# MLP second product as seven block products of Strassen's kind in three of four pairs of groups

## The chip, the cores and the metric

The kernel runs on one core of a Trainium2 chip. The metric is device microseconds (us) of one execution, lower is better. Three runs of the kernel before took 1183.5, 1185.58 and 1185.76 us, so its median is 1185.58 us. The profile is of one further execution.

## The reference, cut to what matters

A decoder trunk of two layers on 512 tokens of width 1024, all in fp32. Layer 0 mixes with gated linear attention, layer 1 with stick-breaking attention; behind each mixer and behind each MLP stands a LayerNorm on `ALPHA * h + mix`. The change touches the MLP alone, which is the same in both layers:

```python
D_MODEL = 1024
SEQ = 512
D_FF = 4 * D_MODEL
...
def sq_relu_mlp(x, w_up, w_down):
    h = jax.nn.relu(x @ w_up)
    return (h * h) @ w_down
...
        h = layer_norm(DEEPNORM_ALPHA * h + sq_relu_mlp(h, mlp_w_up[layer], mlp_w_down[layer]),
                       ln_g[layer, 1], ln_b[layer, 1])
```

The second product is (512 tokens x 4096 features) by (4096 features x 1024 columns).

## The kernel before, in words

**Three matmuls for one product.** Operands are kept as two fp32r parts: `hi` is the value rounded by ScalarE (ACT), `lo` is the rest, subtracted by VectorE (DVE). `mm3` (L85 to L89) sums hi x hi, hi x lo and lo x hi in one PSUM bank. A weight piece is 512 KB: `split_piece` (L62) loads it with SyncE's queue (SP) into one of 3 `raw` buffers, ACT writes `hi` (L67), DVE writes `lo` (L69), 128 x 1024 elements each, into 6 buffers of either kind. `put` (L91) does the same for a computed tile.

**The MLP.** `mlp` (L513) cuts the 4096 features into 8 groups of 512. `up(g)` (L522) makes a group: 96 matmuls of 128 x 512 (four weight pieces, four banks), relu on ACT (L540), the square on DVE (L541) and the split by `put` into 128 x 512 pieces. `down(g)` (L545) takes two groups, a pair: for each half of the 1024 columns it loads four pieces, and sums over both groups in four banks, one per 128 tokens, 12 matmuls per group and bank. So a pair's `down` has 192 matmuls and eight pieces. When a bank is done, DVE adds it to the rows `h` of the residual stream (L161; L159 for the first pair, which scales by ALPHA too), eight adds a pair. The order is up 0, 1, 2, down of pair 0, up 3, up 4, down of pair 2, and so on (L586 to L594): one `up` always lies between a group's matmuls and the `down` that reads it. The last pair is different, since the LayerNorm follows each 128 tokens there.

**What sets the order.** The code is recorded by a framework with a scheduler; each engine then runs its list strictly in order, and tile pools make an instruction wait for the last user of a buffer. PSUM has 8 banks, all from one pool (L53). `unit` (L58) gives 8 buffers of four 128 x 512 tiles, tag `T`; four of them hold the MLP's input. 

Of the kernel before, what the change touches and what calls it, by code (L numbers as in the profile page):

```python
# [34 lines left out]
def yoco_kernel(ctx: ExitStack, tc: tile.TileContext, x, gla_w_in, gla_w_a2, gla_b_a, gla_norm_g,  # L35
                gla_w_o, kv_w, sb_w_q, sb_w_o, mlp_w_up, mlp_w_down, ln_g, ln_b, out):
    nc = tc.nc
# [10 lines left out]
    def nm(s):  # L48
        uid[0] += 1
        return f"{s}{uid[0]}"  # L50

    def bank():
        return psp.tile([P, 512], F32, tag="b", name=nm("ps"))  # L53

    def row_tile():
        return big.tile([P, D], F32, tag="h", bufs=4, name=nm("h"))

    def unit(dtype):  # L58
        return big.tile([P, 4, 512], dtype, tag="T", bufs=8, name=nm("T"))


    def split_piece(src, a):  # L62
        raw = wts.tile([P, 1024], F32, tag="raw", bufs=3, name=nm("raw"))
        v = lambda w: w.rearrange("p (a b) -> p a b", a=a)
        nc.sync.dma_start(out=v(raw), in_=src)
        hi = wts.tile([P, 1024], F32R, tag="hi", bufs=6, name=nm("hi"))
        nc.scalar.activation(hi, raw, AF.Copy)  # L67
        lo = wts.tile([P, 1024], F32R, tag="lo", bufs=6, name=nm("lo"))
        nc.vector.tensor_tensor(lo, raw, hi.bitcast(F32), op=ALU.subtract)  # L69
        return v(hi), v(lo)  # L70

    def pieces_512(w, r0, nkt, c0):

        got = []
        for kp in range(nkt // 2):
            hi, lo = split_piece(
                w[r0 + 256 * kp:r0 + 256 * kp + 256, c0:c0 + 512].rearrange("(a p) c -> p a c", p=P), 2)
            got += [(hi[:, 0, :], lo[:, 0, :]), (hi[:, 1, :], lo[:, 1, :])]
        return got

    def piece_128(w, c0):
        hi, lo = split_piece(w[:, c0:c0 + 128].rearrange("(a p) c -> p a c", p=P), 8)
        return [(hi[:, k, :], lo[:, k, :]) for k in range(8)]

    def mm3(ps, a, b, first, last):  # L85

        nc.tensor.matmul(ps, lhsT=a[0], rhs=b[0], start=first, stop=False)  # L87
        nc.tensor.matmul(ps, lhsT=a[0], rhs=b[1], start=False, stop=False)  # L88
        nc.tensor.matmul(ps, lhsT=a[1], rhs=b[0], start=False, stop=last)  # L89

    def put(hi, lo, ps, keep=lambda ins: ins):  # L91
        keep(nc.scalar.activation(hi, ps, AF.Copy))
        keep(nc.vector.tensor_tensor(lo, ps, hi.bitcast(F32), op=ALU.subtract))  # L93
# [191 lines left out]
    xs, pss = [row_tile() for _ in range(NT)], [bank() for _ in range(NT)]  # L285
    pcs = []
# [7 lines left out]
    for u in range(2):  # L294
        for t in range(NT):
            nc.sync.dma_start(out=xs[t][:, 512 * u:512 * u + 512],
                              in_=x2[128 * t:128 * t + 128, 512 * u:512 * u + 512])
# [3 lines left out]
            raw, hi, lo = (w[:, 512 * (t % 2):512 * (t % 2) + 512] for w in trio)  # L301
            k = 4 * u + t
# [19 lines left out]
    for k in range(8):  # L322
# [3 lines left out]
    a1 = gtp.tile([P, S], F32R, name="a1")  # L326
    nc.scalar.activation(a1[:CH, :], ps[:CH, :], AF.Identity, bias=onerow)
    nc.vector.scalar_tensor_tensor(a1[CH:, :], ps[:CH, :], onerow, a1[:CH, :].bitcast(F32), op0=ALU.add,
                                   op1=ALU.subtract)
    pcs = pieces_512(w_in, 0, 8, 2 * QK + 512)  # L330
    for h in range(GH):
        ps = rows(xT, h, pcs, K8)
        put(vT[1][0][:, h, :], vT[1][1][:, h, :], ps)
        ps = bank()
        c = slice(128 * h, 128 * h + 128)
# [151 lines left out]
    onT.grow()  # L487
    gate(0, 1, pcs)
# [6 lines left out]
    hs = [Rows() for _ in range(NT)]  # L495
# [3 lines left out]
    pcs = pieces_512(gla_w_o[0], 0, 8, 0)  # L499
# [5 lines left out]
    pcs = pieces_512(gla_w_o[0], 0, 8, 512)  # L505
# [5 lines left out]
    NG = DFF // 512  # L511

    def mlp(l, hT, late, vec, done):  # L513


        ml = tc.tile_pool(name=nm("mlp"), bufs=1, reuse_waits="tile")
        mlp_ = ml.__enter__()

        def work():
            return mlp_.tile([P, 512], F32, tag="w2", bufs=6, name=nm("w"))  # L520

        def up(g):  # L522
            pcs = pieces_512(mlp_w_up[l], 0, 8, 512 * g)
            pss = [bank() for _ in range(4)]
            for c0, cn in ((0, 256), (256, 256)) if g == 0 else ((0, 512),):
                for k in range(8):
                    if g == 0 and c0 == 0 and k == 4:
                        late(work)
                    for f in range(4):
                        mm3(pss[f][:, c0:c0 + cn], tuple(w[:, 128 * f:128 * f + 128] for w in pcs[k]),  # L530
                            hT.k(k, c0, cn), k == 0, k == 7)
            if g % 3 == 2:
                sq = Split(0)
                for parts in (sq.hi, sq.lo):
                    parts.append(mlp_.tile([P, 4, 512], F32R, tag="U", bufs=2, name=nm("U")))
            else:
                sq = Split(1)
            for f in range(4):
                r, s2 = work(), work()
                nc.scalar.activation(r, pss[f], AF.Relu)  # L540
                nc.vector.tensor_tensor(s2, pss[f], r, op=ALU.mult)  # L541
                put(sq.hi[0][:, f, :], sq.lo[0][:, f, :], s2)
            return sq

        def down(g, sqs):  # L545

            first, last = g == 0, g == NG - 2

            def into(ps, t, i, pcs, c=slice(0, 512)):
                for k in range(4):  # L550
                    mm3(ps, sqs[i].k(k, 128 * t, 128), tuple(w[:, c] for w in pcs[4 * i + k]),
                        (i, k) == (0, 0), (i, k) == (1, 3))

            for n in range(1 if last else 2):
                pcs = pieces_512(mlp_w_down[l], 512 * g, 8, 512 * n)
                pss = [bank() for _ in range(NT)]
                for i in range(2):
                    for t in range(NT):
                        into(pss[t], t, i, pcs)
                        if i == 1:  # L560
                            hs[t].add(n, pss[t], first, last and not (l == 1 and t == NT - 1))
                            if last and l == 1 and t == NT - 1:
                                for q in range(2):
                                    hs[t].stat(0, q, hs[t].h[:, 256 * q:256 * q + 256], 2)
            if not last:
                return None
            pcs = pieces_512(mlp_w_down[l], 512 * g, 8, 512)

            def mm(t):
                if l == 0 or t < NT - 1:  # L570
                    ps = bank()
                    for i in range(2):
                        into(ps, t, i, pcs)
                    hs[t].add(1, ps, False, True)
                    return

                for q in range(2):
                    ps = bank()[:, 0:256]
                    for i in range(2):
                        into(ps, t, i, pcs, slice(256 * q, 256 * q + 256))  # L580
                    h = hs[t].h[:, 512 + 256 * q:768 + 256 * q]
                    nc.vector.tensor_tensor(h, ps, h, op=ALU.add)
                    hs[t].stat(1, q, h, 2)
            return done(mm, work)

        sqs = [up(0), up(1)]  # L586
        for h in hs:
            h.affine(vec)
        for g in range(0, NG, 2):
            if g + 2 < NG:  # L590
                sqs.append(up(g + 2))
            got = down(g, sqs[g:g + 2])
            if g + 3 < NG:
                sqs.append(up(g + 3))  # L594
        ml.__exit__(None, None, None)
        return got

# [2 lines left out]
    def done0(mm, work):  # L600
        h2T.grow()
        h2T.grow()
        return finish(mm, lncols(0, 1), hs, h2T, work)

    late = mlp(0, hT, late, vec, done0)


# [22 lines left out]
    for n in range(2):  # L630
        pcs = pieces_512(kv_w, 0, 8, D + 512 * n)
# [88 lines left out]
    parts = [(oA.hi[0][:, i, :], oA.lo[0][:, i, :]) for i in range(4)]  # L720
# [6 lines left out]
    for p in range(NP):  # L727
# [4 lines left out]
        else:  # L732
            n = p - (NP - 2)
            pcs = pieces_512(sb_w_o[0], 0, 4, 512 * n)
# [29 lines left out]
    def done1(mm, work):  # L764
# [40 lines left out]
```

## Time and profile before

| what | value |
|---|---|
| profiled execution, device time | 1185.81 us |
| its span, first to last instruction | 1183.9 us |
| granted TensorE clock, mean | 0.999 |
| TensorE (PE) busy | 1167.5 us, 99% of the span, 5629 instructions |
| VectorE (DVE) busy | 635.1 us, 54%, 846 instructions |
| ScalarE (ACT) busy | 458.7 us, 39%, 754 instructions |
| GpSimd (POOL) busy | 96.5 us, 8%, 159 instructions |
| memory traffic | 112.41 MB in DMA packets, mean 95 GB/s |
| DVE's share in the middle of layer 0's MLP (296 to 340 us) | 18.19 of 44.00 us |

How to read it: the profile gives for each engine its busy time, and for each group of instructions the source line, the mean duration and what ended the idle time ahead of them. Matmuls are pipelined, so one lasts longer than the distance to the next; what counts is the distance from start to start. In rows of the profile, `out<-in` names tiles without their numbers, `128*128 128x512` is the weight tile and then the output's partitions and elements.

### The profile page before, as it was taken

Reading aid. Unit: us, or ns where it says so; the run is one execution under the profiler, and the core shown is the slowest. Engines: PE = TensorE matmul, PEld = TensorE weight load, DVE = VectorE, ACT = ScalarE, POOL = GpSimd, SP = SyncE. Lnnn points to the kernel's source line nnn. Section 1 sums busy time; section 2 is a strip of 40 time slices with the busy share of each in tenths; the row PEclk is TensorE's granted clock in tenths of the full one; section 3 lists DMA queues with packets and bytes.
Section 4 is the critical chain, followed back from the end, with each engine's and each line's share of the span. In section 5 each row is a group of like instructions: output and inputs, shape, how many; then the busy total and the mean of one; then the engine's idle time right before and its main releaser. Section 6 shows DMA issues by size and latency. Waiting matters only on the chain.

```text
span 1183.9 us, 14158 instructions
## 1 busy us (share of the span) xinstructions
PE 1167.5 (99%) x5629; PEld 967.8 (82%) x5629; DVE 635.1 (54%) x846; ACT 458.7 (39%) x754; POOL 96.5 (8%) x159
## 2 busy tenths in 40 slices
PE   8999999999999999999999999999999999999997
PEld 7788888898888888888888877778988888888886
DVE  4577545753434434335735878778734344244346
ACT  4455333543323224223635666755433133233220
POOL 1011100100000000000101444330000000000001
PEclk9999999999999999999999999999999999999999
DMA  7441124342333232232244121211532322323212
GB/s 228 122 125 54 36 90 149 99 143 92 102 93 107 89 105 91 89 107 86 75 125 125 54 71 38 71 36 38 177 107 73 119 94 89 108 90 99 96 36 71
DMA packets 82949, 112.41 MB, mean 95 GB/s; under 512 B 11010, under 2 KB 36738, under 8 KB 82884
## 3 DMA queue, kind: packets, MB, share of 16 engines
q1 hardware_dynamic: 82884, 111.52, 30.7%
q8 instruction: 44, 0.72, 0.3%
q14 instruction: 21, 0.17, 0.0%
HBM read 109.41 MB, written 2.10 MB: 94 GB/s over the span
## 4 chain that ended last, share of the span: by engine, by line
PE 83%; DVE 11%; ACT 2%; issue 2%; POOL 1%; DMA 0%; SPq 0%; DVEq 0%; POOLq 0%; ACTq 0%
PE ps L87 27%; PE ps L88 27%; PE ps L89 27%; DVE r L686 4%; DVE lo L69 2%; ACT wt L701 1%; DVE h L187 1%; DVE ps L678 1%; DVE T L93 1%; DVE qs L661 1%; ACT hi L67 1%; PE ps L115 1%; DVE bst L169 1%; POOL rs L177 1%; PE ps L413 0%
## 5 line engine op out<-in xcount | busy, mean ns | idle before, releaser
L69 DVE TENSOR_TENSOR lo<-raw,hi 128x1024 fp32r<-128x1024 f32 x188 | 230.4, 1227 | 338.6 <-ACT hi L67 334.8
L67 ACT ACTIVATE hi<-raw 128x1024 fp32r<-128x1024 f32 x188 | 199.7, 1065 | 448.3 <-PE ps L89 237.0
L87 PE MATMUL ps<-T,hi 128*128 128x512 f32 (+1 forms) x768 | 288.7, 376 | 0.0
L89 PE MATMUL ps<-T,lo 128*128 128x512 f32 (+1 forms) x768 | 285.5, 372 | 0.0
L88 PE MATMUL ps<-T,hi 128*128 128x512 f32 (+1 forms) x768 | 285.4, 372 | 0.0
L87 PE MATMUL ps<-hi,T 128*128 128x512 f32 (+1 forms) x712 | 279.4, 393 | 0.0
L89 PE MATMUL ps<-hi,T 128*128 128x512 f32 (+1 forms) x712 | 276.6, 388 | 0.0
L88 PE MATMUL ps<-lo,T 128*128 128x512 f32 (+1 forms) x712 | 276.4, 388 | 0.0
L89 PEld LDWEIGHTS ps<-T,lo 128*128 128x128 f32 x768 | 144.7, 188 | 25.0
L87 PEld LDWEIGHTS ps<-T,hi 128*128 128x128 f32 x768 | 144.7, 188 | 24.5 <-issue 1.1
L88 PEld LDWEIGHTS ps<-T,hi 128*128 128x128 f32 x768 | 144.8, 189 | 23.6
L89 PEld LDWEIGHTS ps<-hi,T 128*128 128x128 f32 x712 | 134.2, 189 | 27.8 <-DVE T L93 0.2
L87 PEld LDWEIGHTS ps<-hi,T 128*128 128x128 f32 x712 | 134.3, 189 | 27.4 <-issue 1.3
L88 PEld LDWEIGHTS ps<-lo,T 128*128 128x128 f32 x712 | 134.4, 189 | 26.8 <-DVE lo L93 0.3
L177 POOL TENSOR_TENSOR rs<-ve,mhalf 128x1 f32<-128x1 f32 x16 | 12.8, 800 | 816.8 <-DVE ve L175 816.8
L161 DVE TENSOR_TENSOR h<-ps,h 128x512 f32<-128x512 f32 x55 | 37.9, 689 | 56.4 <-PE ps L89 56.3
L686 DVE TENSOR_TENSOR_SCAN r<-r,begin 128x512 f32<-128x512 f32 x40 | 66.2, 1663 | 0.2
L541 DVE TENSOR_TENSOR w<-ps,w 128x512 f32<-128x512 f32 x64 | 43.5, 687 | 28.1 <-ACT w L540 28.1
L687 POOL TENSOR_TENSOR w<-w,r 128x512 f32<-128x512 f32 x40 | 51.4, 1286 | 75.7 <-DVE r L686 60.5
L540 ACT ACTIVATE w<-ps 128x512 f32<-128x512 f32 x64 | 37.4, 592 | 39.3 <-PE ps L89 38.2
L87 PE MATMUL ps<-hi,U 128*128 128x512 f32 x128 | 49.8, 389 | 0.0
L88 PE MATMUL ps<-lo,U 128*128 128x512 f32 x128 | 49.8, 389 | 0.0
(144 smaller groups left out, 974.2 us busy)
## 6 DMA issues: line engine op xcount, KB each, us to landing
raw<-in_mlp_w_up_dram SPq DMA_DIRECT2D x64, 512.0 KB, 3.7
raw<-in_mlp_w_down_dram SPq DMA_DIRECT2D x64, 512.0 KB, 3.5
raw<-in_gla_w_in_dram SPq DMA_DIRECT2D x20, 512.0 KB, 3.9
raw<-in_kv_w_dram SPq DMA_DIRECT2D x16, 512.0 KB, 4.3
raw<-in_gla_w_o_dram SPq DMA_DIRECT2D x8, 512.0 KB, 5.0
raw<-in_sb_w_q_dram SPq DMA_DIRECT2D x8, 512.0 KB, 3.9
raw<-in_sb_w_o_dram SPq DMA_DIRECT2D x8, 512.0 KB, 3.5
h<-in_x_dram SPq DMA_DIRECT2D x8, 256.0 KB, 4.9
```

Source lines behind the costliest of these rows:

```text
L67: nc.scalar.activation(hi, raw, AF.Copy)
L69: nc.vector.tensor_tensor(lo, raw, hi.bitcast(F32), op=ALU.subtract)
L87: nc.tensor.matmul(ps, lhsT=a[0], rhs=b[0], start=first, stop=False)
L88: nc.tensor.matmul(ps, lhsT=a[0], rhs=b[1], start=False, stop=False)
L89: nc.tensor.matmul(ps, lhsT=a[1], rhs=b[0], start=False, stop=last)
L93: keep(nc.vector.tensor_tensor(lo, ps, hi.bitcast(F32), op=ALU.subtract))
L161: nc.vector.tensor_tensor(h, ps, h, op=ALU.add)
L177: nc.gpsimd.tensor_tensor(rs, ve, mhalf[:, 0:1], op=ALU.pow)
L540: nc.scalar.activation(r, pss[f], AF.Relu)
L541: nc.vector.tensor_tensor(s2, pss[f], r, op=ALU.mult)
L686: nc.vector.tensor_tensor_scan(down, down, begins[kind][:, ::-1], 1.0, op0=ALU.mult, op1=ALU.max)
L687: nc.gpsimd.tensor_tensor(w, w, r[:, 1:S + 1], op=ALU.mult)
```

## The change

For three of the four pairs of groups (0, 2 and 4) in each layer, `down` no longer sums eight blocks of a 2 x 2 by 2 x 2 block product, but forms seven products of sums, in Winograd's arrangement. The blocks: tokens in two halves of 256, the pair's two groups as the two halves of the features, columns in two halves of 512. A block product is 2 banks (128 tokens each) x 4 feature tiles x 3 matmuls = 24 matmuls of 128 x 512, so a pair has 168.

- `up` leaves its squares unsplit in fp32, one tile of four 128 x 512 (`s2`, 3 buffers).
- `down` loads the pair's weights as eight fp32 tiles `B` (8 buffers), each four blocks in two halves of 256 features, and forms eight sums of B tiles (128 x 1024) and four sums of squares (128 x 4 x 256) on DVE, most of them in place. Products take their operands split: seven splits of squares by `put` and twelve of B tiles; the sixth product loads a block of weights afresh, two more pieces through `raw`.
- Three sets of two banks carry partial sums: `ys` is opened by the first product and goes on in the third, fifth and seventh, `xs` belongs to the second, `zs` is opened by the fourth and goes on in the sixth. After each product DVE adds the bank as it stands to the rows that it belongs to (14 adds a pair), and the next product of that set sums on in the bank that was read. `start` and `stop` are set at the first and last matmul of a set only.
- The last pair (`down_last`) is computed as before; its first group is split while the products of the pair ahead run. The scratch tile `work()`, used by the LayerNorm code too, is now a quarter of an `s2` tile, 3 buffers for 6.

```diff
+        def four():
+            return mlp_.tile([P, 4, 512], F32, tag="s2", bufs=3, name=nm("s2"))
...
-            return mlp_.tile([P, 512], F32, tag="w2", bufs=6, name=nm("w"))
+            return four()[:, 0, :]
...
+            s2 = four()
             for f in range(4):
-                r, s2 = work(), work()
-                nc.scalar.activation(r, pss[f], AF.Relu)
-                nc.vector.tensor_tensor(s2, pss[f], r, op=ALU.mult)
-                put(sq.hi[0][:, f, :], sq.lo[0][:, f, :], s2)
+                nc.scalar.activation(s2[:, f, :], pss[f], AF.Relu)
+                nc.vector.tensor_tensor(s2[:, f, :], pss[f], s2[:, f, :], op=ALU.mult)
+            return s2
...
+        def down(g, a1, a2):
+            tt = nc.vector.tensor_tensor
+            first, last = slice(0, 256), slice(256, 512)
+            a11, a21, a12, a22 = a1[:, :, first], a1[:, :, last], a2[:, :, first], a2[:, :, last]
+            bs = []
+            for h in range(2):
+                four_b = []
+                for k, j in ((1, 1), (0, 1), (0, 0), (1, 0)):
+                    b = mlp_.tile([P, 1024], F32, tag="B", bufs=8, name=nm("B"))
+                    nc.sync.dma_start(out=b.rearrange("p (a b) -> p a b", a=2),
+                                      in_=block(mlp_w_down[l], 512 * (g + k) + 256 * h, 512 * j))
+                    four_b.append(b)
+                bs.append(four_b)
+            sums = unit(F32)
+            s1, s2 = sums[:, :, first], sums[:, :, last]
+            tt(s1, a21, a22, op=ALU.add)
+            tt(s2, s1, a11, op=ALU.subtract)
+            for b22, b12, b11, b21 in bs:
+                tt(b22, b22, b12, op=ALU.subtract)
+                tt(b12, b12, b11, op=ALU.subtract)
...
+            def product(a, b, banks, opens, closes, i, j):
+                for s in range(2):
+                    if opens:
+                        banks[s] = bank()
+                    for k in range(4):
+                        for x, y in ((0, 0), (0, 1), (1, 0)):
+                            nc.tensor.matmul(banks[s], lhsT=a(k, s)[x], rhs=b[k][y],
+                                             start=opens and (k, x, y) == (0, 0, 0),
+                                             stop=closes and (k, x, y) == (3, 1, 0), skip_group_check=True)
+                    hs[2 * i + s].add(j, banks[s], (i, j) not in done)
+                done.add((i, j))
+
+            product(split_a(a11), split_b(2), ys, True, False, 0, 0)
+            tt(a21, a11, a21, op=ALU.subtract)
+            product(split_a(a12), split_b(3), xs, True, True, 0, 0)
+            tt(a12, a12, s2, op=ALU.subtract)
+            for b22, b12, b11, b21 in bs:
+                tt(b11, b22, b11, op=ALU.add)
+                tt(b21, b21, b11, op=ALU.subtract)
+            product(split_a(s2), split_b(2), ys, False, False, 0, 1)
+            product(split_a(s1), split_b(1), zs, True, False, 1, 1)
+            product(split_a(a21), split_b(0), ys, False, False, 1, 1)
+            product(split_a(a12), pieces_512(mlp_w_down[l], 512 * (g + 1), 4, 512), zs, False, True, 0, 1)
+            product(split_a(a22), split_b(3), ys, False, True, 1, 0)
...
-        sqs = [up(0), up(1)]
+        sq = [up(0), up(1)]
...
+        for g in range(0, NG - 2, 2):
+            sq.append(up(g + 2))
+            down(g, *sq[g:g + 2])
+            if g < NG - 4:
+                sq.append(up(g + 3))
+        sqs = [parts(sq[NG - 2]), parts(up(NG - 1))]
+        got = down_last(NG - 2, *sqs)
```

The new code puts DVE's work for the products among its older work. These are DVE's rows in the first `down` of layer 0 before, from the fourth square of the third `up` (names: `w` the square or relu, `U` the split square, `lo` a piece's low part, `h302` to `h305` the rows of the four token tiles, `ps` a bank):

```order
L541 TENSOR_TENSOR w457_2588<-ps447_2470,w456_2587 128x512
L93 TENSOR_TENSOR U449_2568<-w455_2582,U448_2567 128x512
L69 TENSOR_TENSOR lo479_2731<-raw477_2727,hi478_2729 128x1024
L93 TENSOR_TENSOR U449_2568<-w457_2588,U448_2567 128x512
L69 TENSOR_TENSOR lo482_2737<-raw480_2733,hi481_2735 128x1024
L69 TENSOR_TENSOR lo485_2743<-raw483_2739,hi484_2741 128x1024
L159 SCALAR_TENSOR_TENSOR h302_1607<-h302_1607,ps470_2617 128x512
L159 SCALAR_TENSOR_TENSOR h303_1608<-h303_1608,ps471_2618 128x512
L159 SCALAR_TENSOR_TENSOR h304_1609<-h304_1609,ps472_2619 128x512
```

And these are DVE's rows in the same `down` now, from the add of the first product's first bank to that of the third product's second bank (`ps445` and `ps446` are `ys`, `ps452` and `ps453` `xs`; `T459` and `T466` the split squares of products four and five, `T471` of product six; `B517` belongs to the next pair):

```order
L165 SCALAR_TENSOR_TENSOR h302_1607<-h302_1607,ps445_2576 128x512
L72 TENSOR_TENSOR lo461_2691<-B432_2544,hi460_2689 128x1024
L165 SCALAR_TENSOR_TENSOR h303_1608<-h303_1608,ps446_2590 128x512
L99 TENSOR_TENSOR T459_2686<-T439_2558,T459_2686 128x4x256
L72 TENSOR_TENSOR lo463_2695<-B436_2552,hi462_2693 128x1024
L167 TENSOR_TENSOR h302_1607<-ps452_2616,h302_1607 128x512
L99 TENSOR_TENSOR T466_2725<-s2396_2251,T466_2725 128x4x256
L167 TENSOR_TENSOR h303_1608<-ps453_2630,h303_1608 128x512
L72 TENSOR_TENSOR lo468_2730<-B431_2542,hi467_2728 128x1024
L72 TENSOR_TENSOR lo470_2734<-B435_2550,hi469_2732 128x1024
L165 SCALAR_TENSOR_TENSOR h302_1607<-h302_1607,ps445_2576 128x512
L99 TENSOR_TENSOR T471_2762<-s2413_2384,T471_2762 128x4x256
```

What moved: an add and the splits for the product three places on now alternate, so an add can stand behind two splits, and a split behind an add that waits for PE.

On PE, this is where the second product ends and the third goes on in `ps445`, the bank that the first product filled and DVE read (in brackets what a row waits for; the twelve matmuls of a bank are merged where they repeat):

```order
L592 MATMUL ps453_2630<-hi450_2612,T447_2605 128x512 x2
L592 MATMUL ps453_2630<-lo451_2614,T447_2605 128x512
L592 MATMUL ps453_2630<-hi450_2612,T447_2605 128x512
L592 MATMUL ps445_2576<-hi455_2652,T454_2649 128x512 [waits DVE_49,Activation_49]
L592 MATMUL ps445_2576<-lo456_2654,T454_2649 128x512
```

Before, a bank of `down` went on after a pause only at the second group, and had not been read in between; only splits were waited for there:

```order
L89 MATMUL ps473_2620<-hi462_2601,T397_2252 128x512
L87 MATMUL ps470_2617<-hi465_2607,T422_2401 128x512 [waits Activation_49]
L88 MATMUL ps470_2617<-lo466_2609,T422_2401 128x512 [waits DVE_49]
L89 MATMUL ps470_2617<-hi465_2607,T423_2402 128x512
L87 MATMUL ps470_2617<-hi465_2607,T422_2401 128x512
```

The wait for DVE at a product's start covers the add of that bank and the low part of the operands; between the end of the first product's bank and this row stand 36 other matmuls (12 in `ps446`, 24 in the second product).

On SP's queue at the head of each MLP the eight B loads now stand among the pieces of `up`: seven of them are issued ahead of the second weight piece of the third `up`. Outside the two MLPs the order on every engine is what it was.

More of the change, by code (lines that the diff above doesn't have):

```diff
@@ L63, in split_piece, with split_tile @@
         raw = wts.tile([P, 1024], F32, tag="raw", bufs=3, name=nm("raw"))
+        nc.sync.dma_start(out=raw.rearrange("p (a b) -> p a b", a=a), in_=src)
+        return split_tile(raw, a)
+    def split_tile(raw, a):
         v = lambda w: w.rearrange("p (a b) -> p a b", a=a)
-        nc.sync.dma_start(out=v(raw), in_=src)
         hi = wts.tile([P, 1024], F32R, tag="hi", bufs=6, name=nm("hi"))
@@ L70, in split_piece, with block @@
         return v(hi), v(lo)
+    def block(w, r0, c0):
+        return w[r0:r0 + 256, c0:c0 + 512].rearrange("(a p) c -> p a c", p=P)
     def pieces_512(w, r0, nkt, c0):
@@ L75, in pieces_512 @@
         for kp in range(nkt // 2):
-            hi, lo = split_piece(
-                w[r0 + 256 * kp:r0 + 256 * kp + 256, c0:c0 + 512].rearrange("(a p) c -> p a c", p=P), 2)
+            hi, lo = split_piece(block(w, r0 + 256 * kp, c0), 2)
             got += [(hi[:, 0, :], lo[:, 0, :]), (hi[:, 1, :], lo[:, 1, :])]
@@ L531, in up @@
                             hT.k(k, c0, cn), k == 0, k == 7)
[L532 to L537, printed above, removed]
-            for f in range(4):
-                r, s2 = work(), work()
-                nc.scalar.activation(r, pss[f], AF.Relu)
-                nc.vector.tensor_tensor(s2, pss[f], r, op=ALU.mult)
-                put(sq.hi[0][:, f, :], sq.lo[0][:, f, :], s2)
@@ L543, in up, with split_a, split_b @@
-            return sq
-        def down(g, sqs):
-            first, last = g == 0, g == NG - 2
+            s2 = four()
+            for f in range(4):
+                nc.scalar.activation(s2[:, f, :], pss[f], AF.Relu)
[21 more added lines that the diff above has]
+                tt(b12, b12, b11, op=ALU.subtract)
+            def split_a(a):
+                u = unit(F32R)
+                put(u[:, :, first], u[:, :, last], a)
+                return lambda k, s: (u[:, k, 128 * s:128 * s + 128], u[:, k, 256 + 128 * s:384 + 128 * s])
+            def split_b(i):
+                got = []
+                for h in range(2):
+                    hi, lo = split_tile(bs[h][i], 2)
+                    got += [(hi[:, 0, :], lo[:, 0, :]), (hi[:, 1, :], lo[:, 1, :])]
+                return got
+            done = set() if g == 0 else {(i, j) for i in range(2) for j in range(2)}
+            ys, xs, zs = ([None, None] for _ in range(3))
+            def product(a, b, banks, opens, closes, i, j):
[21 more added lines that the diff above has]
+            product(split_a(a22), split_b(3), ys, False, True, 1, 0)
@@ L549, in into, with parts, down_last @@
+        def parts(a):
+            sq = Split(1)
+            for f in range(4):
+                put(sq.hi[0][:, f, :], sq.lo[0][:, f, :], a[:, f, :])
+            return sq
+        def down_last(g, *sqs):
             def into(ps, t, i, pcs, c=slice(0, 512)):
@@ L552, in into @@
                         (i, k) == (0, 0), (i, k) == (1, 3))
[L554 to L566, printed above, removed]
+            pcs = pieces_512(mlp_w_down[l], 512 * g, 8, 0)
+            pss = [bank() for _ in range(NT)]
+            for i in range(2):
+                for t in range(NT):
+                    into(pss[t], t, i, pcs)
+                    if i == 1:
+                        hs[t].add(0, pss[t], False, not (l == 1 and t == NT - 1))
+                        if l == 1 and t == NT - 1:
+                            for q in range(2):
+                                hs[t].stat(0, q, hs[t].h[:, 256 * q:256 * q + 256], 2)
             pcs = pieces_512(mlp_w_down[l], 512 * g, 8, 512)
@@ L584, in down @@
             return done(mm, work)
-        sqs = [up(0), up(1)]
+        sq = [up(0), up(1)]
         for h in hs:
             h.affine(vec)
[L589 to L594, printed above, removed]
+        for g in range(0, NG - 2, 2):
[5 more added lines that the diff above has]
+        got = down_last(NG - 2, *sqs)
         ml.__exit__(None, None, None)
```

## The prediction

> **What bounds the kernel now.** I read the page first: the engines' shares, the granted clock by slice, and the chain that ended last.
>
> ```profile
> span 1183.9 us, 14158 instructions
> ...
> PE 1167.5 (99%) x5629; PEld 967.8 (82%) x5629; DVE 635.1 (54%) x846; ACT 458.7 (39%) x754; POOL 96.5 (8%) x159
> ...
> PEclk9999999999999999999999999999999999999999
> ...
> PE 83%; DVE 11%; ACT 2%; issue 2%; POOL 1%; DMA 0%; SPq 0%; DVEq 0%; POOLq 0%; ACTq 0%
> ```
>
> PE is busy all the time and makes up 83% of the chain. A busy PE alone says little, because matmuls overlap, so I asked next who made PE wait (the waits of PE: us in total, times, longest), and looked at the stretches of the MLP itself (columns: length, then busy time of PE, weight loads, DVE, ACT, POOL, granted clock, DMA share, GB/s).
>
> ```profile
> PE ps L696 <- POOL w L687: 3.1, 5, 1.7
> PE ps L205 <- DVE h L181: 2.4, 3, 0.9
> PE ps L115 <- DMA h<-in_x_dram: 2.0, 2, 1.3
> PE ps L292 <- POOL ident L125: 1.6, 1, 1.6
> ...
> 296.00:340.00 44.00, 44.00 (x196) 36.44 (x195) 18.19 (x22) 11.53 (x16) 0.00 (x0) 1.00 0.31 95
> 340.00:384.00 44.00, 44.00 (x196) 36.44 (x195) 17.28 (x20) 14.73 (x20) 0.00 (x0) 1.00 0.33 106
> 384.00:428.00 44.00, 44.00 (x196) 36.44 (x195) 17.61 (x22) 11.50 (x14) 0.00 (x0) 1.00 0.28 86
> ```
>
> PE waited 9.1 us in all, none of it for a product of the MLP (L696 is attention, L205 a LayerNorm's transposes, the other two the start). In the MLP it has no idle time, at full clock, while DVE is busy 40%. So there a matmul costs its distance to the next. The timeline gives it: the first matmul of layer 0's first down (columns: start, duration) and the first of the up behind it.
>
> ```profile
> 297.34 0.39 PE L87 MATMUL ps<-hi,T 128*128 128x512 f32 x1
> ...
> 340.86 0.39 PE L87 MATMUL ps<-T,hi 128*128 128x512 f32 x1
> ```
>
> 192 matmuls lie between: 43.52 us, or 226.7 ns each, nothing lost at the places where PE waited for new weight pieces.
>
> **What the change removes.** A pair has 168 matmuls for 192; six pairs are changed (three in each layer), so 6 x 24 = 144 matmuls of 128 x 512 go. The new ones have the same shape, operands and sequence of three, so they keep the pace: 144 x 226.7 ns = **32.6 us** off PE's path, if PE waits nowhere anew.
>
> The Trainium skill ("TensorE: Matmul & The Clock Gate", section "Wait — 56ns, not 53.3ns?") gives 215.7 ns from start to start for 512 columns at full clock. By that the sum would be 144 x 215.7 = 31.1 us; the trace's 226.7 ns is for these very fp32r matmuls, so the measured one decides.
>
> **What it adds, and what covers it.** The prices, from the groups by line:
>
> ```profile
> L69 DVE TENSOR_TENSOR lo<-raw,hi 128x1024 fp32r<-128x1024 f32 x188 | 230.4, 1227 | 338.6 <-ACT hi L67 334.8
> ...
> L67 ACT ACTIVATE hi<-raw 128x1024 fp32r<-128x1024 f32 x188 | 199.7, 1065 | 448.3 <-PE ps L89 237.0
> ...
> L93 DVE TENSOR_TENSOR T<-w,T 128x512 fp32r<-128x512 f32 x66 | 44.7, 683 | 0.4
> ...
> L541 DVE TENSOR_TENSOR w<-ps,w 128x512 f32<-128x512 f32 x64 | 43.5, 687 | 28.1 <-ACT w L540 28.1
> ...
> L161 DVE TENSOR_TENSOR h<-ps,h 128x512 f32<-128x512 f32 x55 | 37.9, 689 | 56.4 <-PE ps L89 56.3
> ...
> L686 DVE TENSOR_TENSOR_SCAN r<-r,begin 128x512 f32<-128x512 f32 x40 | 66.2, 1663 | 0.2
> ...
> L92 ACT ACTIVATE T<-w 128x512 fp32r<-128x512 f32 x66 | 41.5, 633 | 3.1 <-DVE w L541 2.2
> ...
> L540 ACT ACTIVATE w<-ps 128x512 f32<-128x512 f32 x64 | 37.4, 592 | 39.3 <-PE ps L89 38.2
> ...
> 831.38 2.35 DVE L69 TENSOR_TENSOR lo<-raw,hi 128x1024 fp32r<-128x1024 f32 x2
> ```
>
> DVE per pair (two ups, one down) before: 16 pieces x 1.227 + 8 squares x 0.687 + 8 splits of squares x 0.683 + 8 adds x 0.689 = 36.1 us; the windows above show 34.9 us in 88, so the prices hold. Now: 8 pieces of up (9.8), 8 squares (5.5), 12 sums, 14 weight splits and 7 splits of squares, all of 1024 elements (33 x 1.227 = 40.5), 14 adds (9.6): **65.4 us**. No row shows a sum of two B tiles or a 128 x 4 x 256 operand. The nearest is L69, two SBUF inputs and 1024 elements; from below, two of them back to back took 2.35 us, so the second adds 1.13; from above stands L686's 1.663, the dearest two-input row. I take 1.227. PE now needs (192 + 168) x 226.7 ns = 81.6 us a pair, so DVE is 80% full, still not the bound. ACT per pair: 8 x 0.592 + 29 x 1.065 = 35.6 us (before 26.8), under half of PE.
>
> The total hides the queue. DVE takes its list in order, and in the down phase, 168 x 0.2267 = 38.1 us, it stands close to full: from the first add to the last it has 14 adds and 21 operations of 1024 elements, 14 x 0.689 + 21 x 1.227 = 35.4 us. So I walked the new order through one down, with PE's products 5.44 us apart (24 matmuls), a bank 2.72, each DVE row starting behind the row ahead, its PE bank, and ACT's high part:
>
> - Operands. Product four starts at 16.3 us after the first; its last split (the low part beside `T459`'s) is done at 9.6. For five, six and seven: 14.6, 20.9 and 25.9, wanted at 21.8, 27.2 and 32.6. The next up's first piece is done at 31, wanted at 38.1. Nothing is nearer than **6 us**.
> - Banks that are gone on with. The add is late by at most 3.5 us (product six, second bank: it ends at 32.6, the add is done at 36.1). Between a bank's end and the next matmul into it lie 36 matmuls, 36 x 0.2267 = 8.2 us. So **4.7 us** are spare, and a read bank costs PE nothing. From below: PE has no idle time here that a gain could come from.
> - At the start of a down, its first products' sums and splits lie behind the squares of the up before the last: 4 squares, then some 15 rows of up to 1.23 us, about 21 us, beside an up of 96 x 0.2267 = 21.8 us; what product one reads is done after 8 us. Product three's last split comes 4 us into the down, wanted at 12.
>
> The rest is off the path. SP issues two more loads a pair, all of the size known:
>
> ```profile
> raw<-in_mlp_w_up_dram SPq DMA_DIRECT2D x64, 512.0 KB, 3.7
> raw<-in_mlp_w_down_dram SPq DMA_DIRECT2D x64, 512.0 KB, 3.5
> ...
> 237.28 0.37 SPq L65 DMA_DIRECT2D raw<-in_mlp_w_up_dram  x1
> ...
> 237.00:242.00 5.00, 5.00 (x44) 5.00 (x43) 5.00 (x10) 3.34 (x9) 0.00 (x0) 1.00 0.54 107
> 242.00:247.00 5.00, 5.00 (x44) 5.00 (x43) 1.30 (x3) 1.06 (x1) 0.00 (x0) 1.00 0.71 213
> ...
> 253.80 0.40 PE L87 MATMUL ps<-T,hi 128*128 128x512 f32 x1
> ```
>
> 18 loads of 0.52 MB in 81.6 us are 116 GB/s, for 16 in 87.0 (96) before. At the head of the MLP seven B loads and a piece go out together where before only that piece did (237.28, the row above): 4.2 MB, at the 213 GB/s of the window shown 20 us, so until 258; the next piece, the third up's second, lands at 260. DVE's B sums there wait for these loads, with the second up's last two pieces queued behind them until 250 and 257. The second up starts at 253.8 (row above), wants these at 264.7 and 270.1, and the third up wants its second piece at 281.0. Cover of 12 us and more, so nothing; if it were gone, see the third rival. The three scratch buffers for six and the split of the last pair's first group (4 rows of 0.68 us in a phase that has 4.7 us to spare) cost nothing either.
>
> **Sum**, against the profiled execution's own time of 1185.81 us: 1185.81 - 32.6 = **1153.2 us**. That execution lies 0.2 us above the median of the three runs, so the same for it.
>
> **Rivals.**
>
> 1. *DVE becomes the bound.* For it: 35.4 of 38.1 us in the down, and the unseen forms. If all operations of 1024 elements took L686's 1.663 us, a pair would need 41 x 1.663 + 15.2 = 83.3 us of DVE against 81.6 of PE: 6 x 1.7 = 10.4 us back, **1163.6**. Against it: the same engine does the same kind of subtraction in 1.227, in 188 cases. Chance 0.07.
> 2. *PE waits at each bank it goes back to (slower).* Four products a pair go on in a read bank, so 48 banks in all. If PE stood at each until DVE had read it just then, it would lose the hand-over and the add. The row shows an add 0.40 us after DVE was free, waiting for PE:
>
> ```profile
> 311.14 0.69 DVE L159 SCALAR_TENSOR_TENSOR h<-h,ps 128x512 f32<-128x512 f32 x1 [0.40 <-PE ps L89]
> ```
>
>    The bank's last matmul starts at 297.34 + 59 x 0.2267 = 310.72, so 1.1 us from there to the add's end, 0.9 beyond the next start: 48 x 0.9 = 43 us, **1196**. It decides once DVE is 8.2 us behind, for then adds, not splits, are what PE meets; at 0.68 us a bank the whole gain is gone. The walk says 3.5. Were PE's clock to fall to half after such waits, over the 24 products entered this way, 24 x 5.44 = 131 us would come on top of the forecast, 1284; the clock row above, 9 in every slice, the ones with PE's waits among them, speaks against it. Chance 0.03, of which 0.005 for the clock.
>    The Trainium skill (same page, section "A second HAM failure mode: psum-queue depth-cycling") has that rule: a PE that idles briefly between groups of matmuls while it cycles through banks drops to half its clock again and again. No row here bears it out.
> 3. *The B loads at the head hold back the third up.* At only the span's mean of 95 GB/s the nine loads up to its second piece, 4.7 MB, take 50 us: landed at 287.4, split at 290, wanted at 281.0. 9 us in each layer, **1171**. Against it: 213 GB/s above. Chance 0.03.
> 4. *It does not do what it says*, the products costing PE what the removed matmuls did (by a slower pace beside a fuller DVE): 226.7 ns would have to become 259 in the 1008 matmuls of the products. **1185.8**, chance 0.02.
>
> **How the numbers follow.** The forecast has the remaining 0.85: 1153.2. Its own spread: the three runs before lie 2.3 us apart, so down to 1150.9; upwards the unseen forms, half of the first rival's price, to 1158.5. That holds the forecast and a part of rival one, and leaves out less than 0.2. What a measurement can tell from no change is 0.2%, 2.4 us: faster 0.95 (forecast, rivals one and three), same 0.02, slower 0.03.
>
> **What would show it.** In the changed kernel's profile: PE with 5485 instructions; 226.7 ns between matmuls in the products; an up and a down together 59.9 us in place of 65.3; DVE busy about 35 of 44 us where it was 18; no wait of PE for DVE or ACT in the MLP; adds late by under 4 us; sums at 1.1 to 1.25 us. Wrong would be: sums at 1.6 us (rival one), PE's waits naming the add's line (two), PE waiting for a piece of up near 281 us (three), a longer pace (four), each with the time given.

## The result, and the profile after

The changed kernel takes 1151.8 us (median of four runs, 1151.31 to 1153.02), the kernel before 1185.38 us (four runs, 1183.5 to 1185.76): ratio 0.9721, 95% interval 0.9705 to 0.9738. The forecast was 1153.2. The profiled execution took 1152.1 us. Its page (span, busy times, granted clock) and the waits of PE:

```profile
span 1150.4 us, 14083 instructions
...
PE 1133.6 (99%) x5485; PEld 939.9 (82%) x5485; DVE 795.9 (69%) x984; ACT 513.9 (45%) x784; POOL 96.5 (8%) x159
...
PEclk9999999999999999999999999999999999999999
```

```profile
PE ps L764 <- POOL w L755: 3.1, 5, 1.7
PE ps L121 <- DMA h<-in_x_dram: 2.5, 2, 1.3
PE ps L211 <- DVE h L187: 2.4, 3, 0.9
PE ps L298 <- POOL ident L131: 1.6, 1, 1.6
```

The list of waits is that of before under new line numbers: attention, start, LayerNorm, no product. PE has 144 instructions less and is as full as it was; DVE has 161 us more to do and no product waits for it. The span fell by 33.5 us, PE's busy time by 33.9.

PE's timeline, at the first product, the first matmul of the up behind it and the first product of the next pair (columns: start, duration):

```profile
296.62 0.39 PE L592 MATMUL ps<-hi,T 128*128 128x512 f32 x1
...
334.70 0.39 PE L93 MATMUL ps<-T,hi 128*128 128x512 f32 x1
...
378.22 0.39 PE L592 MATMUL ps<-hi,T 128*128 128x512 f32 x1
```

168 matmuls in 334.70 - 296.62 = 38.08 us are 226.7 ns each, as before; a pair takes 81.60 us, 24 x 0.2267 = 5.44 us less than before. The stretches of one pair, down, two ups, and both (length, busy time of PE, weight loads, DVE, ACT, POOL, clock, DMA share, GB/s):

```profile
296.80:334.90 38.10, 38.10 (x169) 31.55 (x169) 33.75 (x37) 19.12 (x19) 0.00 (x0) 1.00 0.51 170
334.90:378.40 43.50, 43.50 (x193) 36.04 (x192) 27.80 (x28) 15.59 (x19) 0.00 (x0) 1.00 0.22 69
296.80:378.40 81.60, 81.60 (x361) 67.59 (x361) 61.55 (x64) 34.70 (x38) 0.00 (x0) 1.00 0.36 116
```

DVE is busy 33.8 of 38.1 us in the down, and never the one that PE waits for. Its timeline in this down shows how close it comes:

```profile
306.06 0.68 DVE L167 TENSOR_TENSOR h<-ps,h 128x512 f32<-128x512 f32 x1
...
308.39 2.35 DVE L72 TENSOR_TENSOR lo<-B,hi 128x1024 fp32r<-128x1024 f32 x2
...
314.13 2.35 DVE L72 TENSOR_TENSOR lo<-raw,hi 128x1024 fp32r<-128x1024 f32 x2
...
320.05 1.22 DVE L72 TENSOR_TENSOR lo<-B,hi 128x1024 fp32r<-128x1024 f32 x1
```

Counted from 296.62, the fifth product's operands are there at 14.1 us (308.39 + 2.35), the sixth's at 19.9, the seventh's at 24.7, for 21.8, 27.2 and 32.6. The latest add of the down is the first row: the second product's first bank ends at 296.62 + 36 x 0.2267 = 304.78, the add begins 1.3 us behind that and is done 2.0 us behind it.

### The profile page after: what moved, and what is told of

The parts are those of the page before. It is cut to its first block, busy times and chain, and to the rows that moved or that the text cites. A ratio compares the mean times of both kernels' runs of the same rounds, so it can differ in the third digit from the quotient of the medians.

```text
span 1150.4 us, 14083 instructions
## 1 busy us (share of the span) xinstructions
PE 1133.6 (99%) x5485; PEld 939.9 (82%) x5485; DVE 795.9 (69%) x984; ACT 513.9 (45%) x784; POOL 96.5 (8%) x159
## 4 chain that ended last, share of the span: by engine, by line
PE 83%; DVE 11%; ACT 2%; issue 2%; POOL 1%; DMA 0%; SPq 0%; DVEq 0%; POOLq 0%; ACTq 0%
PE ps L93 20%; PE ps L592 20%; PE ps L94 20%; PE ps L95 20%; DVE r L754 4%; DVE lo L72 2%; ACT wt L769 1%; DVE h L193 1%; DVE ps L746 1%; DVE T L99 1%; DVE qs L729 1%; ACT hi L70 1%; PE ps L121 1%; DVE bst L175 1%; POOL rs L183 1%
## 5 line engine op out<-in xcount | busy, mean ns | idle before, releaser
L72 DVE TENSOR_TENSOR lo<-raw,hi 128x1024 fp32r<-128x1024 f32 x152 | 185.3, 1226 | 156.2 <-ACT hi L70 154.3
L70 ACT ACTIVATE hi<-raw 128x1024 fp32r<-128x1024 f32 x152 | 161.7, 1067 | 238.0 <-PE ps L94 109.5
L592 PE MATMUL ps<-hi,T 128*128 128x512 f32 x672 | 207.9, 389 | 0.0
L93 PE MATMUL ps<-hi,T 128*128 128x512 f32 (+1 forms) x456 | 179.2, 393 | 0.0
L95 PE MATMUL ps<-hi,T 128*128 128x512 f32 (+1 forms) x456 | 176.8, 388 | 0.0
L94 PE MATMUL ps<-lo,T 128*128 128x512 f32 (+1 forms) x456 | 176.6, 387 | 0.0
L592 PEld LDWEIGHTS ps<-hi,T 128*128 128x128 f32 x672 | 126.1, 188 | 26.3
L592 PE MATMUL ps<-lo,T 128*128 128x512 f32 x336 | 130.7, 389 | 0.0
L70 ACT ACTIVATE hi<-B 128x1024 fp32r<-128x1024 f32 x72 | 76.3, 1059 | 109.3 <-PE ps L94 75.3
L72 DVE TENSOR_TENSOR lo<-B,hi 128x1024 fp32r<-128x1024 f32 x72 | 87.5, 1222 | 46.2 <-ACT hi L70 45.8
L95 PEld LDWEIGHTS ps<-hi,T 128*128 128x128 f32 x456 | 85.9, 188 | 17.7 <-DVE T L99 0.3
L93 PEld LDWEIGHTS ps<-hi,T 128*128 128x128 f32 x456 | 86.1, 189 | 17.4 <-issue 1.3
L167 DVE TENSOR_TENSOR h<-ps,h 128x512 f32<-128x512 f32 x91 | 62.4, 686 | 20.7 <-PE ps L95 20.5
```

The source lines that it names most:

```text
L592: nc.tensor.matmul(banks[s], lhsT=a(k, s)[x], rhs=b[k][y], start=opens and (k, x, y) == (0, 0, 0), stop=closes and (k, x, y) == (3, 1, 0), ...
```

## Experiments

The theory: PE's pace sets the time, so the gain is the number of matmuls removed, and it holds as long as DVE's queue comes to operands and banks in time. Against it stood three doubts: that part of the gain is something else, that a return to a read bank costs PE something, and that DVE's share of the time, not its order, is what counts. Medians below stand beside 1151.8 to 1151.9 us for the changed kernel, which was also run again (last table row).

| run | us | PE waits for operands or banks in the MLPs |
|---|---|---|
| eighth product | 1184.34 | none |
| bank resumed at once | 1200.04 | 37.1 us, 24 times |
| order 1, 3, 2, 4, 6, 5, 7 | 1152.09 | none |
| no return | 1151.85 | none |
| 7 DVE operations more a down | 1151.93 | none |
| 14 more | 1158.44 | 3.8 us, twice |
| 21 more | 1230.15 | 47.5 us, 24 times |
| fourth pair | 1155.06 | 4.3 us, twice |
| fourth pair, covered | 1150.15 | none |
| fourth pair, transposes later | 1146.60 | none |
| the changed kernel again | 1151.85 | none |

**The matmuls put back, the staging kept.**

```diff
+            a_2, b_2 = split_a(a12), split_b(3)
-            product(split_a(a12), split_b(3), xs, True, True, 0, 0)
+            product(a_2, b_2, xs, True, True, 0, 0)
+            product(a_2, b_2, [None, None], True, True, 0, 0, False)
...
```

The last argument, `False`, says that DVE adds these two banks to nothing.

> The second product of each of the six downs is run once more into two banks of its own that nothing reads (24 matmuls more a down, 144 in all; nothing else is added, and the staging with its sums, splits and adds stays). Theory (PE's pace sets the time and the staging costs nothing): 144 x 0.2267 us = 32.6 us more, 1151.8 + 32.6 = 1184.4 us, within 1.5 us of the kernel before (1185.4); 226.7 ns from matmul to matmul. Rival (a part of the gain came from the staging, such as fewer adds in the way or other banks): the time ends clearly under 1184, by that part. Rival (the staging costs PE something that the gain covers): the spare product gives slack to DVE, so the time rises by less than 32.6 us.

1184.34 us, 32.5 above the changed kernel and level with the kernel before on the same chip (1184.87; ratio 0.9996, 0.9987 to 1.0005). So 144 matmuls account for the whole gain; all the sums, splits, adds and B loads cost nothing that can be measured, nor do they bring anything.

**The return to a read bank.** Products are taken half by half (here 1 and 3, the other pairs cut), and the order of the products' matmuls on PE is kept:

```diff
-            product(split_a(a11), split_b(2), ys, True, False, 0, 0)
+            x = (split_a(a11), split_b(2), ys, True, False, 0, 0)
...
+            y = (split_a(s2), split_b(2), ys, False, False, 0, 1)
+            for s in range(2):
+                half(s, *x)
+                half(s, *y)
...
```

> The same 168 matmuls a down in another order: products 1 and 3, 4 and 6, 5 and 7 are taken half by half, so that PE goes back at once to a bank whose partial sum DVE has still to read (6 such returns a down, 36 in all), and this order of PE is kept. Theory (the second rival of the prediction had the right price, and the gap of 8.2 us between a bank's end and its return is what saves it): PE stands at each return for the add and the hand-over, 0.9 us or more, longer where the add stands behind other work of DVE: 36 x 0.9 = 32 us or more, 1184 us and above, with rows of waits of PE for the line of the adds. Rival (a return to a read bank costs PE nothing, the hand-over being hidden somehow): 1152. Rival (PE's clock falls to half behind such waits): up to 36 x 12 x 0.2267 = 98 us on top, and a granted clock under 1 in the downs.

1200.04 us, 48 above the changed kernel (the profiled execution took 1196.55). The waits of PE at this kernel's products, then two rows of its timeline:

```profile
PE ps L592 <- DVE h L167: 24.8, 16, 1.9
PE ps L592 <- DVE h L165: 12.3, 8, 1.9
```

```profile
317.26 0.39 PE L592 MATMUL ps<-hi,T 128*128 128x512 f32 x1
318.52 0.47 PE L592 MATMUL ps<-hi,T 128*128 128x512 f32 x1 [0.87 <-DVE h L165]
```

The wait names the lines of the add, as the second rival said. Where the add was next in DVE's queue, start to start is 1.26 us for 0.23: 1.03 us lost. Where another operation stood ahead of it, 1.8 to 2.1 us (waits of 1.65 to 1.95). Only 24 of the 36 returns wait; at the other 12, between products 5 and 7, the scheduler put 7 to 9 matmuls of the next up into the gap. From start to start, the 24 returns lose 41 us in the profiled execution. The rival with the half clock came about behind one return of the 24, in layer 1; why there alone, the last section shows.

> The order of the products is 1, 3, 2, 4, 6, 5, 7 in place of 1 to 7: a bank is resumed one half product (12 matmuls, 2.7 us) after its end in place of three (8.2 us). Theory: adds end 0.4 to 1.7 us late plus 0.69 us of their own, so under 2.7 us: mostly hidden, 0 to 8 us more, 1152 to 1160 us; PE waits for the adds, if any, under 0.3 us each. Rival (each return costs PE something whatever the gap): as in the kernel with returns at once, 1184 or more.

Edit: the same seven products in the order 1, 3, 2, 4, 6, 5, 7. 1152.09 us and no wait: 2.7 us between a bank's end and its return are as good as 8.2.

> Each product opens and closes two banks of its own, so no bank is gone back to; DVE adds each product to every block that it belongs to, 28 adds a down in place of 14 (14 x 0.69 = 9.7 us more of DVE a down). PE has the same 168 matmuls. Theory (DVE counts by its queue in the down, 33.8 us of 38.1 there): the added 9.7 us go past what is left there, the seventh product's operands come at 24.7 + 8.3 = 33 us for 32.6, so 0 to 2 us a down: 1152 to 1164 us, DVE busy near 71 us of a pair. Rival (only DVE's total in a pair counts, 71 of 81.6 us): 1152. Rival (the returns to read banks cost PE something even now): faster than 1150.

```diff
-                    if opens:
-                        banks[s] = bank()
+                    ps = bank()
...
-                    hs[2 * i + s].add(j, banks[s], (i, j) not in done)
...
+                    for i, j in outs:
+                        hs[2 * i + s].add(j, ps, (i, j) not in done)
```

1151.85 us: neither slower by the 14 adds nor faster without returns. So in the changed kernel the returns cost nothing, and neither the theory's upper end (1164) nor "faster than 1150" came about. DVE is busy 69.9 us of a pair here.

**How much room DVE has.** In `split_a`, which runs seven times a down, the low part is made n times more (n is 1, 2 and 3):

```diff
                 put(u[:, :, first], u[:, :, last], a)
+                for _ in range(n):
+                    tt(u[:, :, last], a, u[:, :, first].bitcast(F32), op=ALU.subtract)
```

> The subtraction that makes the low part of each product's left operand (1024 elements, two inputs) is issued once more on DVE: 7 more a down, 7 x 1.13 to 1.22 = 8 to 8.5 us. Theory (what counts is when DVE's queue comes to the operands, with 3 of the 7 falling into the up before): product 7's operands at 24.7 + 4 x 1.13 = 29.2 us for 32.6: no wait, 1152. Upper end, if all 7 fall into the down: 24.7 + 7.9 = 32.6 for 32.6, at most 0.5 us a down, 1155. Rival (only DVE's total in a pair counts, 69.5 of 81.6): 1152. Rival (DVE is the bound already): 6 x 8 = 48 us more, 1200.

> The same subtraction twice more: 14 more operations of 1024 elements a down, 15.8 to 17 us. Theory (queue in the down): with 6 of them in the up before, product 7's operands at 24.7 + 8 x 1.13 = 33.7 us for 32.6, and the next up's first piece late by as much: 1 to 2 us a down, 1158 to 1164; if all fall into the down, up to 8.5 us a down, 1203. Rival (DVE's total, 77.4 of 81.6 us): 1152. Waits of PE for splits in the downs under the theory, none under the rival.

> The same subtraction three times more: 21 more operations a down, 23.7 to 25.6 us. Theory (queue in the down): product 6's operands at 19.9 + 9 x 1.13 = 30.1 for 27.2, product 7's at 24.7 + 12 x 1.13 = 38.3 us for 32.6: 5.7 us a down or more, 1186 and above. Rival (DVE's total, 85.3 of 81.6 us): 6 x 3.7 = 22 us, 1174, with waits spread over ups and downs.

Measured 1151.93, 1158.44 and 1230.15 us. With 7 more no product waits, as theory and rival both had it. Stretches of a whole pair, with 14 more (two pairs) and then with 21 more (columns as above; DVE's time is the third):

```profile
296.80:378.40 81.60, 81.60 (x362) 67.59 (x361) 76.78 (x78) 34.73 (x38) 0.00 (x0) 1.00 0.36 116
378.40:460.00 81.60, 81.60 (x362) 67.59 (x361) 76.79 (x78) 34.73 (x38) 0.00 (x0) 1.00 0.36 116
```

```profile
322.66:417.44 94.78, 86.86 (x360) 70.25 (x360) 84.84 (x85) 34.59 (x37) 0.00 (x0) 0.95 0.31 100
417.44:512.53 95.09, 87.18 (x360) 70.59 (x360) 84.89 (x85) 34.91 (x38) 0.00 (x0) 0.95 0.23 75
```

With 14 more, DVE is 94% busy and PE still loses nothing in these pairs: my theory, which wanted a microsecond or two in every down, has the right sum in the wrong place, and by luck: nearly half of the loss is a slower clock, which the theory did not have. The loss is one wait of 1.9 us in each layer, behind the third down, where the last up's piece is late, and what follows it. With 21 more, DVE needs 84.8 us for 81.6, the rival's 85.3. By that rival a pair would grow by 3 us; it grows by 13, while DVE is idle for 10 of the 94.8. So neither view holds alone. Up to 94% the scheduler moved enough of the work into the ups: of the 15.2 us that DVE has more in such a pair, 11.2 lie in its two ups (39.0 us for 27.8). Past 100% the price is more than the excess, and no run separates what sets the length of each wait there. Part of the price is in the clock. PE's timeline, 14 more, behind the third down:

```profile
499.54 0.39 PE L594 MATMUL ps<-hi,T 128*128 128x512 f32 x1
501.84 1.19 PE L95 MATMUL ps<-T,lo 128*128 128x512 f32 x4 [1.92 <-DVE lo L72]
502.87 0.43 PE L93 MATMUL ps<-T,hi 128*128 128x512 f32 x1
503.11 0.63 PE L94 MATMUL ps<-T,hi 128*128 128x512 f32 x1
503.53 0.63 PE L95 MATMUL ps<-T,lo 128*128 128x512 f32 x1
...
506.09 0.59 PE L95 MATMUL ps<-T,lo 128*128 128x512 f32 x1
506.51 0.39 PE L93 MATMUL ps<-T,hi 128*128 128x512 f32 x1
```

A microsecond behind the wait, eight matmuls from 503.11 to 506.51 stand 0.425 us apart in place of 0.227, then the old pace is back: 3.4 us at half speed, 1.6 us lost beside the 2.1 of the wait itself. The windows show it as granted clock:

```profile
502.00:504.00 2.00, 2.00 (x8) 1.58 (x9) 2.00 (x2) 0.00 (x0) 0.00 (x0) 0.77 0.52 121
504.00:506.00 2.00, 2.00 (x6) 1.61 (x5) 0.05 (x1) 0.00 (x0) 0.00 (x0) 0.50 0.88 316
```

3.7 us in each of two layers make 7.4, for 6.5 by the medians and 7.8 by the spans. With 21 more, waits of 2.90 and 3.51 us come in each of the three downs of layer 0, and a stretch at half speed, of 3.4 or 6.8 us, begins during or behind each of the six, as it does in layer 1:

```profile
326.06 1.22 PE L594 MATMUL ps<-hi,T 128*128 128x512 f32 x2 [2.90 <-DVE T L575]
327.08 0.63 PE L594 MATMUL ps<-lo,T 128*128 128x512 f32 x1
327.51 1.05 PE L594 MATMUL ps<-hi,T 128*128 128x512 f32 x2
```

Its span is 80.0 us longer than the changed kernel's: 47.5 us of waits, and PE's busy time 1166.7 for 1133.6, 33 us more for the same matmuls.

**A fourth pair.** 24 matmuls more can go, if layer 0's last pair takes seven products too; there the LayerNorm has to follow.

```diff
+        if l == 0:
+            sq.append(up(NG - 1))
+            seventh = down(NG - 2, *sq[NG - 2:], True)
...
```

> In layer 0 the last pair of groups too takes seven products (24 matmuls less; layer 1's last pair stays as it was). The LayerNorm that was woven into the last pair's rows then stands behind products 6 and 7: rows 0 and 1 are complete behind the sixth, rows 2 and 3 behind the seventh. Theory (PE's count of matmuls, where DVE's queue is not late): 24 x 0.2267 = 5.4 us less, 1151.8 - 5.4 = 1146.4, if the LayerNorm of rows 2 and 3 hides behind the transposes of rows 0 and 1 and the next product. Rival (the operands of the second product and the LayerNorm stand in DVE's queue behind the squares of the up just before, since no other up lies between it and the down): 1 to 8 us of waits of PE there, with the slower clock behind a wait of 2 us, 1147 to 1156 us.

1155.06 us, 3.2 slower than the changed kernel run beside it. Its waits of PE:

```profile
PE ps L592 <- ACT T L98: 2.4, 1, 2.4
...
PE ps L592 <- DVE T L99: 1.9, 1, 1.9
PE ps L211 <- DVE ve L181: 1.7, 1, 1.7
```

The rival's mechanism, though at the first product and not at the second that it named: no up lies between this down and its operands. The first product waits 2.4 us and again 1.9 for the two parts of its operand, with half speed from 522.63 to 529.46 us around the second wait. So the queues were rearranged: B sums and the first product's operands ahead of the last up, the second's ahead of the A sums, the LayerNorm between the halves of the seventh product.

```diff
+            if end:
+                a_1, b_1 = split_a(a11), split_b(2)
+                a2 = up(NG - 1)
+                a12, a22 = a2[:, :, first], a2[:, :, last]
+                a_2, b_2 = split_a(a12), split_b(3)
...
+            norm(0)
+            norm(1)
+            seventh(0)
+            turn(0, work)
+            norm(2)
+            seventh(1)
+            turn(1, work)
+            norm(3)
+            turn(2, work)
```

> The fourth pair's version with its waits covered: in layer 0's last down the B loads, the B sums and the first product's operands are written ahead of the last up, the second product's operands ahead of the A sums, and the LayerNorm is written row by row between the two halves of the seventh product. Theory (the fourth pair was slower only because operands and LayerNorm stood late in DVE's and ACT's queues, 2.4 and 1.9 us of waits with the slow clock behind them, and 1.7 us at the LayerNorm): these go, and 24 x 0.2267 = 5.4 us stay: 1146.4 to 1148.5 us. Rival (the pair without an up beside it has more work for DVE than PE can cover): waits come back at a later product, 1151 us or more.

1150.15 us, between the theory's times and the rival's. No product waits any more, but PE waits for the LayerNorm, and half speed again goes with it (562.33 to 569.16 us). The LayerNorm's row among the waits of PE in this kernel:

```profile
PE ps L211 <- DVE h L187: 4.7, 4, 2.7
```

Last, `turn(2)` and `turn(3)`, the transposes of rows 2 and 3, went behind the first two products of the next stage:

```diff
-            turn(2, work)
-            got = lambda work: turn(3, work)
+            got = [lambda work: turn(2, work), lambda work: turn(3, work)]
...
```

> As the covered version of the fourth pair, and the transposes of rows 2 and 3 behind layer 0's LayerNorm stand behind the first and the second product of the next stage, so that PE has 5.4 us of other work ahead of each. Theory (the 2.7 us wait of PE for the LayerNorm's scaling and the ten half-speed matmuls behind it, 2.0 + 0.5 + 1.8 us of PE's time, are what the fourth pair still loses): they go, 1150.2 - 4.3 = 1145.9 us, from 1145 to 1147. Rival (the LayerNorm's chain is late wherever it stands): 1149 us or more, with PE waiting in a later transpose or product.

1146.6 us (1145.59 to 1147.07), ratio 0.9677 (0.9663 to 0.969) to the kernel before. Its waits of PE, in which the wait of 2.7 us is gone (the last row is in the stage behind the MLP):

```profile
PE ps L807 <- POOL w L798: 2.8, 4, 1.7
PE ps L121 <- DMA h<-in_x_dram: 2.1, 2, 1.7
PE ps L211 <- DVE h L187: 1.9, 3, 0.9
PE ps L298 <- POOL ident L131: 1.6, 1, 1.6
PE ps L94 <- DVE lo L72: 0.4, 1, 0.4
```

24 matmuls of 0.2267 us are 5.4 us; it is 5.25 us faster than the changed kernel. The same 24 matmuls less gave 3.2 us more, 1.7 less and 5.25 less, and what differs between the three is what stood ahead of the operands and of the LayerNorm. The last is the fastest version here.

## Why the prediction was right, point by point

- **The count and the pace.** 144 matmuls at 226.7 ns: right to the third digit, in the timeline and in the run with the eighth product (32.5 us for 32.6). By the 215.7 ns of the Trainium skill ("TensorE: Matmul & The Clock Gate", section "Wait — 56ns, not 53.3ns?") it would be 31.1 us, 1.4 off that run. The spans differ by 0.9 us more, 33.5; 0.7 of that was there ahead of the first MLP, where the LayerNorm's transposes begin at 221.10 us for 221.82. It is there already at PE's 33rd matmul, which starts at 12.52 us for 13.28, so it belongs to the start of these two executions and is no part of the change. By the medians the gain is 33.6, 1.0 above the sum, which is within the spread of one kernel's runs (1.7 to 2.3 us). (The range's upper end, 1153.2 + 5.2, should have read 1158.4.)
- **DVE's work of a pair.** 61.6 us for 65.4 predicted. The unseen sums and in-place forms cost what the row of the split did:

```profile
L568 DVE TENSOR_TENSOR B<-B,B 128x1024 f32<-128x1024 f32 x12 | 14.6, 1221 | 4.2 <-DMA B<-in_mlp_w_down_dram 4.2
...
L604 DVE TENSOR_TENSOR B<-B,B 128x1024 f32<-128x1024 f32 x12 | 14.1, 1217 | 0.0
```

  The mis-sized term is the mean itself: two back to back take 2.35 us (308.39 above), so the second adds 1.13, not 1.22. The 41 operations of 1024 elements in a pair would by that be up to 4.0 us less, an estimate, and 3.8 is the difference. The mean of an operation prices a single one; a queue of them is shorter.
- **The walk.** Operands of the fourth to seventh product predicted at 9.6, 14.6, 20.9 and 25.9 us, measured at 9.5, 14.1, 19.9 and 24.7. Adds are done at most 2.0 us behind their bank's end, for 3.5 predicted.
- **The first rival** (DVE bound) had the wrong price per excess. It charged DVE's surplus over PE once; the run with 21 operations more shows 13 us a pair for a surplus of 3. Its mechanism did not occur: there was room for 7 to 14 operations more a down, more than the 4.7 us that I read from the down alone, since the scheduler moves sums and splits into the ups.
- **The second rival** (returns to a bank) had the right price, 1.03 us for 0.9 at a bare hand-over, and the right reason for not coming about. The point at which it would decide was far away: with adds done at most 2.0 us late, a gap of 2.7 us is still enough.
- **The half clock.** I argued from the row of nines that PE's clock does not fall behind waits. That step failed: the clock falls to half at waits of 1.9 us and more in five of these kernels. The row could not have shown it, for each of its digits covers some 30 us: the pages of the kernel with 14 operations more and of the one with returns at once read 9 in every slice too, around slow stretches of 3.4 us. It did no harm to the forecast, since the changed kernel has no such wait in its MLPs; that rests on the walk, not on this argument. The size was off too: 1.6 to some 3 us a wait, not 5.4 a product.
- **The third rival** (B loads at the head): the loads went at up to 347 GB/s, not at the mean of 95 or the 213 that I took, and the third up's second piece, predicted to land at 260 us, was split from 256.3 on. The window of after that lies beside the prediction's:

```profile
242.00:247.00 5.00, 5.00 (x44) 5.00 (x43) 3.59 (x3) 1.06 (x1) 0.00 (x0) 1.00 1.02 347
```

## What to carry to other kernels

Where one engine is full and another half empty, moving work from the first to the second can pay exactly the removed work, as it did here while no operand was late; the second could be filled to 94% in the pairs without a wait of the first. Count the work per stage, but judge the cover by the place in the queue: the same 24 removed matmuls were worth from -3.2 to +5.25 us. A wait of some 2 us on TensorE can cost nearly twice its length (1.92 us cost 3.7 here).

## What the hardware showed that I had not expected

TensorE's clock can fall to half for 3.4 us behind a short wait. The wait of 1.92 us above did it in both layers, and those of 2.90 and 3.51 us did it all twelve times. In the kernel that resumes banks at once, 1.94 us did not:

```profile
296.73 0.39 PE L592 MATMUL ps<-hi,T 128*128 128x512 f32 x1
299.05 0.47 PE L592 MATMUL ps<-hi,T 128*128 128x512 f32 x1 [1.94 <-DVE h L165]
299.36 0.40 PE L592 MATMUL ps<-lo,T 128*128 128x512 f32 x1
```

In its layer 1, though, a wait of 1.95 us (from 988.34 to 990.28) did. The traces show what decides. The slow stretches of an execution begin whole multiples of 3.413 us apart, wherever the waits stand: with 14 operations more at 503.09 and 1086.77 us, 171 multiples. So I cut each execution into windows of that length, on this grid (where an execution has no slow stretch, the clock's fall behind PE's last work sets it), and took PE's idle time in each (length less PE's busy time, the first two numbers of a row; the clock is the third number from the right). First the kernel with returns at once, around its wait of 1.94 us and then its wait of 1.95, then the one with 14 more:

```profile
295.34:298.75 3.41, 1.78 (x8) 1.13 (x6) 3.40 (x4) 0.47 (x1) 0.00 (x0) 1.00 0.06 22
298.75:302.17 3.42, 3.12 (x14) 2.63 (x15) 0.16 (x1) 0.00 (x0) 0.00 (x0) 1.00 0.53 158
988.25:991.66 3.41, 1.47 (x7) 1.19 (x7) 1.88 (x3) 0.00 (x0) 0.00 (x0) 1.00 0.15 55
991.66:995.08 3.42, 3.42 (x10) 2.64 (x9) 1.49 (x2) 0.00 (x0) 0.00 (x0) 0.50 0.28 104
499.67:503.09 3.42, 1.50 (x7) 1.05 (x6) 3.13 (x4) 0.00 (x0) 0.00 (x0) 1.00 0.11 17
503.09:506.50 3.41, 3.41 (x9) 2.64 (x8) 0.96 (x1) 0.00 (x0) 0.00 (x0) 0.50 0.92 273
```

The wait of 1.94 us lies across an edge, 1.64 us of it in one window and 0.30 in the next; those of 1.92 and 1.95 us lie whole in one. Counted so over all 13 profiles, from 14 us on and up to PE's last work, each of the 17 full-clock windows with 1.80 us or more of idle time was followed by one at half clock, and none of the other 4303, with 1.74 us or less. By these traces it is the idle time within one window that counts, summed over waits, and the place of a wait decides between 1.92 and 1.94 us. The kernel before and the changed one come to 1.67 and 1.65 us in attention, not far below.

The Trainium skill ("TensorE: Matmul & The Clock Gate", section "What's actually happening") describes a monitor with a free-running window of 3413 ns, which agrees with the multiples of 3.413 us; its section "HAM oscillation — how this bites in real kernels" puts the idle gap that it takes at over some 3.4 us, and here 1.80 us within one window sufficed. No run moved a wait within its window on purpose: the rule is read off the traces as they are.
